# A hybrid decoder layer: the attention pools of the mixer closed early, a pool of its own for the mixed results, and a second mixer that takes two steps at every tenth call

## The chip, the cores and the metric

The kernel runs on one core of one Trainium2 chip. The metric is the device time of one execution in microseconds (us); of several runs the median is given. Engine names: PE is TensorE (matmuls), DVE is VectorE, ACT is ScalarE, POOL is GpSimd, SP is SyncE, which here only issues DMAs.

## The reference

One decoder layer on 1040 tokens (16 meta tokens and 1024 others) of width 1024, all in float32, then a final norm:

```
h = h + 1/2 * SwiGLU(rmsnorm(h))            # FFN 1, hidden width 2816
p = rmsnorm(h) @ w_in                       # q, k, v (512 columns each) and 1024 columns for the convolution
a = diff_attention(q, k, v)                 # 4 heads, two softmax maps each: (p1 - lam * p2) @ v
a = rmsnorm(a, subln_w) * (1 - lambda_init) # per head
c = swish(layernorm(conv31(GLU(u))))        # causal depthwise convolution, 512 channels
h = h + concat([a, c]) @ w_out
h = h + 1/2 * SwiGLU(rmsnorm(h))            # FFN 2
y = rmsnorm(h), without the meta tokens
```

## The kernel before, in words

**Layout.** Activations stand channel by token: 128 partitions of channels, tokens along the free dimension. Tokens are done in two blocks (b = 0: 528 with the meta tokens, b = 1: 512). Every float32 product is made from a high and a low part of both operands (`split`, L128: ACT casts the high part, DVE subtracts it for the low part) as three matmuls: high by high, high by low, low by high. All of them go through `mm` (L57), so they all carry line L58.

**Order.** FFN 1 on block 0, projection of block 0, FFN 1 on block 1 with the mixer of block 0 (attention and convolution) in the background, projection of block 1, FFN 2 on block 0 with the mixer of block 1 in the background, then the output projection of block 1 and FFN 2 on block 1. "In the background" means a generator: `ffn` calls `step()` (L224, L230, L274) between its pieces, and in the two FFNs with a mixer each call takes the generator `bg` one step on (L819, L1017). Two steps are taken ahead (L1015, L1016).

**An FFN.** For each of 22 slices f of the hidden width, `gate_up` (L191) makes 24 matmuls `pg`, calls `step()`, makes 24 matmuls `pu` and calls `step()` again. After each chunk of slices (4, 4, 4, 2, 4, 4 in FFN 2) `down_piece` makes the `dn` matmuls; after each of the four weight tiles of a chunk there is a call of `step()`. One slice of the next chunk is always made ahead of the down pieces. At the start of the last chunk `ahead()` (L253) is called instead; in FFN 2 on block 0 this is `second_out` (L850).

**The mixer (L767).** Its two halves are stepped together. `att` does four heads; each head has four units of 128 queries (`unit`, L417) and each unit has three steps: scores of the first map (`sc`, a PSUM tile of the pool `psS`, which holds one tile); the transposes of the unit before (`tm`, also in `psS`); the product with the values of an earlier pair of units, if there is one, then the scores of the second map and the softmax. When the heads are through and the two pending pieces are done, `sub_ln` (L516) makes the norm of the four heads: squares, four pairs of matmuls `v`, `rstd` (ten small operations), a store of the result row to DRAM (`rscr`, L525), a load that spreads it over all partitions (`ra`, L528), the product (L529) and `store_ac`. `cnv` does the 31 taps of four channel tiles on DVE (L547), then `conv_ln` (L562): sums, two matmuls, `rstd`, and for each tile L585 to L589 and `store_ac`. The taps and the last part of `conv_ln` are given a priority that is lower by 600 instructions (`LATE`); weight loads (`load_w`, L108) are given one that is higher by 500 (`AHEAD`). The framework that builds the program orders the instructions of each engine and each queue by priority and by when it thinks each can start, and an engine then runs its list in that order.

**`store_ac` (L532)** takes one of the eight result tiles (four heads, four convolution tiles), splits it into a high and a low tile (name `a`, 128 x 512, 256 KB each) and stores both to the DRAM scratch `acscr` from POOL (L536). The two tiles come from the tag `rs` of the pool `tmp`, which has two buffers and also serves the temporaries of `rstd`. `ra` comes from the tag `ssum` of the same pool, two buffers.

```
def store_ac(m, i, src):
    hi, lo = [tmp.tile([P, HB], F32R, tag="rs", name="a") for _ in range(2)]
    split(hi, lo, src)
    for j, t in enumerate((hi, lo)):
        store(acscr[m.b, i, :, j], t.bitcast(F32))
```

**`second_out` (L850)** runs what is left of the mixer, closes the mixer's pools, opens others in that memory, and makes the output projection of block 1 in two halves of 256 tokens. Each half needs all eight result tiles: it loads 16 tiles of 256 KB in all from `acscr` (`acl`, and `ext` for four of the second half, L888), the convolution's first, issued by SP as are all weight loads. It then makes, for each half, 8 groups of 24 matmuls `wo` (128 x 256), from eight weight tiles of 512 KB (`wraw<-wo`, then the split `whl`; 2 + 1 and 4 buffers). The first matmuls of each group take the convolution's tiles. The residual comes in one load of 2 MB (`x<-xscr`, L857).

**Pools (L385).** `mid_pools` opens, on the right end of the memory and one above the other, the pools `qk`, `pt`, `v` (all of attention's tiles) and `tmp` (the heads' results and small ones).

Of the kernel before, what the change touches and what calls it, by code (L numbers as in the profile page):

```python
# [9 lines left out]
F32 = mybir.dt.float32  # L10
F32R = mybir.dt.float32r
# [7 lines left out]
P = 128  # L19
# [16 lines left out]
HB = SEQ // 2  # L36
# [3 lines left out]
FB = [[(0, HM // 2), (HM // 2, HM // 2)], [(0, HB)]]  # L40
# [10 lines left out]
def layer(ctx, tc, xb, wgu1, wd1, win, wv, wo, wgu2, wd2, colv, lamv, consts, cossin, out):  # L51
# [5 lines left out]
    def mm(o, lhsT, rhs, start, stop):  # L57
        T.matmul(o, lhsT, rhs, start=start, stop=stop)  # L58

    def pool(stack, name, bufs, side="left"):  # L60
        return stack.enter_context(tc.tile_pool(name=name, bufs=bufs, side=side, reuse_waits="tile"))
# [6 lines left out]
    tmp = pool(ctx, "tmp", 2)  # L68
# [30 lines left out]
    def col(i):  # L99
        return cols[:, i:i + 1]  # L100
# [4 lines left out]
    def psb(name):  # L105
        return psB.tile([P, 512], F32, tag="b", name=name)
# [21 lines left out]
    def split(dst_hi, dst_lo, src):  # L128
        S.copy(dst_hi, src)  # L129
        return V.tensor_tensor(dst_lo, src, dst_hi.bitcast(F32), op=ALU.subtract)  # L130

    def sq_piece(xs, w, ssum, first):
        if first:
            S.activation(ssum[:, :w], xs, AF.Square)
        else:
            sq = tmp.tile([P, 512], F32, tag="sq", name="sq")
            S.activation(sq[:, :w], xs, AF.Square)
            V.tensor_tensor(ssum[:, :w], ssum[:, :w], sq[:, :w], op=ALU.add)
# [7 lines left out]
    def rstd(var, dst, w, scale=1.0, quick=False):  # L146
        def square(o, i):
            if quick:
                V.tensor_tensor(o, i, i, op=ALU.mult)
            else:  # L150
                S.activation(o, i, AF.Square)

        v = tmp.tile([P, 512], F32, tag="rs", name="rv")[:, :w]
        V.tensor_scalar(v, var, scale, EPS, op0=ALU.mult, op1=ALU.add)
        V.tensor_scalar(dst.bitcast(I32), v.bitcast(I32), -0.5, RSQRT_SEED, op0=ALU.mult, op1=ALU.add)
        q = tmp.tile([P, 512], F32, tag="rs", name="rq")[:, :w]
        square(q, dst)
        V.scalar_tensor_tensor(q, q, -RSQRT_K, v, op0=ALU.mult, op1=ALU.mult)
        V.scalar_tensor_tensor(dst, q, RSQRT_K * RSQRT_C, dst, op0=ALU.add, op1=ALU.mult)
        square(q, dst)  # L160
        V.tensor_tensor(v, q, v, op=ALU.mult)
        V.tensor_scalar(q, v, 0.375, -1.25, op0=ALU.mult, op1=ALU.add)
        V.tensor_tensor(q, q, v, op=ALU.mult)
        V.scalar_tensor_tensor(dst, q, 1.875, dst, op0=ALU.add, op1=ALU.mult)

    def norm_r(dst, w, ssum, late=0, extra=None):
        v = psb("v")
        with tc.high_priority(offset=-late):
            mm(v[:, :w], onesD, ssum[:, :w], True, extra is None)
            if extra is not None:  # L170
                mm(v[:, :w], onesD, extra[:, :w], False, True)
        rstd(v[:, :w], dst, w, quick=extra is not None)
# [212 lines left out]
    def mid_pools(stack, b):  # L385
        m = Mid()
        nk = NM + HB * (b + 1)
        m.b, m.nk = b, nk
        m.qk = pool(stack, f"qk{b}", 2, side="right")
        m.pt = pool(stack, f"pt{b}", 2, side="right")  # L390
        m.v = pool(stack, f"v{b}", 2 - b, side="right")
        m.tmp = pool(stack, f"mt{b}", 2, side="right")
        m.vm = m.v.tile([80, P], F32R, tag="vm", name="vm", bufs=1)
        m.pm = [m.tmp.tile([P, 80], F32R, tag=f"pm{i}", name="pm", bufs=1) for i in range(2)]
        for t in m.pm + [m.vm]:
            V.memset(t.bitcast(F32), 0.0)
        load_vm(m, 0)
        m.accs = {}
        m.os = []
        m.pend = []  # L400
        return m

    def load_vm(m, h):
        for part, row in ((0, 0), (0, 32), (1, 64)):
            dma(m.vm[row:row + NM].bitcast(F32), vscr[0:NM, h, part])
# [110 lines left out]
    def sub_ln(m):  # L516
        v = psb("v")
        for h in range(4):
            sq = tmp.tile([P, 512], F32, tag="sq", name="sq")
            S.activation(sq, m.os[h], AF.Square)  # L520
            mm(v[32 * h:32 * h + 32], onesH, sq, True, True)
        rr = tmp.tile([P, 512], F32, tag="ssum", name="rr")
        rstd(v, rr, 512)
        for h in range(4):
            store(rscr[m.b, h:h + 1], rr[32 * h:32 * h + 1])  # L525
        for h in range(4):
            ra = tmp.tile([P, 512], F32, tag="ssum", name="ra")
            dma(ra, rscr[m.b, h].partition_broadcast(P))  # L528
            V.scalar_tensor_tensor(ra, m.os[h], wsub, ra, op0=ALU.mult, op1=ALU.mult)  # L529
            store_ac(m, h, ra)  # L530

    def store_ac(m, i, src):  # L532
        hi, lo = [tmp.tile([P, HB], F32R, tag="rs", name="a") for _ in range(2)]
        split(hi, lo, src)
        for j, t in enumerate((hi, lo)):
            store(acscr[m.b, i, :, j], t.bitcast(F32))  # L536
# [191 lines left out]
    def finish(x, b):  # L728
        todo = []

        def out_piece(c0, w, dd, gained=False):
            for e in (dd, dd + 1):
                y = x[:, e, c0:c0 + w]
                if gained:
                    V.tensor_tensor(y, y, rB[:, c0:c0 + w], op=ALU.mult)
                else:
                    V.scalar_tensor_tensor(y, y, col(C_GF + e), rB[:, c0:c0 + w], op0=ALU.mult, op1=ALU.mult)
            dma(out[dd * P:(dd + 2) * P, b * HB + c0:b * HB + c0 + w].rearrange("(a p) c -> p a c", a=2),
                x[:, dd:dd + 2, c0:c0 + w])

        sums = [None]

        def f(c0, w, d):
            end = b == 1 and c0 + w == HB
            xs = x[:, d, c0:c0 + w]
            if d == 0:
                sums[0] = tmp.tile([P, 512], F32, tag="ssum", name="ssum")
            extra = None
            if end and d == ND - 1:
                extra = tmp.tile([P, 512], F32, tag="sq", name="sq")  # L750
                S.activation(extra[:, :w], xs, AF.Square)
            else:
                sq_piece(xs, w, sums[0], d == 0)
            if todo and d % 2 == 0:
                out_piece(*todo.pop(0))
            if d == ND - 1:
                if end:
                    for e in range(ND):
                        S.activation(x[:, e, c0:c0 + w], x[:, e, c0:c0 + w], AF.Copy, scale=col(C_GF + e))
                norm_r(rB[:, c0:c0 + w], w, sums[0], extra=extra)  # L760
                todo.extend((c0, w, dd, end) for dd in range(0, ND, 2))
                if end or w == HB:
                    for a in todo:
                        out_piece(*a)
        return f

    def mixer(m, zs):  # L767
        def att():
            for h in range(4):
                yield from head(m, h)  # L770
            while m.pend:
                m.pend.pop(0)()
                yield
            sub_ln(m)

        def cnv():
            for c in range(4):
                yield from conv(m, c, zs[c])
            yield from conv_ln(m)
        a, c = att(), cnv()  # L780
        while True:
            done = next(a, STOP) is STOP
            done = (next(c, STOP) is STOP) and done
            if done:
                break
            yield
# [9 lines left out]
    x = ffn1_first()  # L796
# [10 lines left out]
    x = res.pop()  # L807
    enter(xs)
    es_l.close()
    es_m = ExitStack()  # L810
    bg = mixer(mid_pools(es_m, 0), zs)

    def drain():
# [23 lines left out]
    x = res.pop()  # L837
    enter(xs)
    es_l.close()

    es_m = ExitStack()
    bg = mixer(mid_pools(es_m, 1), zs)
    es_l = ExitStack()
    x1 = []
# [169 lines left out]

    next(bg, None)  # L1015
    next(bg, None)  # L1016
    ffn(FB[1], FB[1], wgu2, wd2, x, finish(x, 0), lambda: next(bg, None), third_in, scaled=True, second=True, ahead=second_out)  # L1017
    ffn(FB[1], [(0, QT), (QT, QT)], wgu2, wd2, x1[0], finish(x1[0], 1), nothing, nothing, second=True, pair_of=gate_up_pair)
    es_l.close()

# [73 lines left out]
```

## Time and profile before

| what | us |
|---|---|
| median of 3 runs (1958.42 to 1961.5) | 1961.13 |
| time of the profiled execution | 1960.6 |
| its span | 1958.8 |
| PE busy in it | 1915.6 (98%) |
| DVE busy | 1416.0 (72%) |
| ACT busy | 770.3 (39%) |
| POOL busy | 70.2 (4%) |

The span is the time from the first to the last instruction of the profiled execution; its own time is 1.8 us longer. Busy times are sums over instructions; an engine that is idle is either waiting for another one or has nothing to do. A busy PE may run at a lower clock: the granted clock is given as a share of full speed (2.4 GHz), and its lower level is half of that.

### The profile page before, as it was taken

How to read it: one execution, taken by the hardware profiler on the slowest of the kernel's cores; microseconds unless marked ns; L12 is line 12 of the kernel's file. 1: busy time of each engine (PE TensorE's matmuls, PEld its weight loads, DVE VectorE, ACT ScalarE, POOL GpSimd, SP SyncE). 2: the span in 40 equal slices, each digit the busy share in tenths (PEclk: the TensorE clock that was granted, in tenths of full speed). 3: DMA queues.
4: the chain of work that ended last, by engine and by line, in shares of the span. 5: the costliest groups of instructions: out<-in, count | busy, mean ns of one | idle time of the engine just before them, and what ended most of it. 6: DMA issues, size and time to landing. Idle time of an engine off the chain costs nothing.

```text
span 1958.8 us, 29371 instructions
## 1 busy us (share of the span) xinstructions
PE 1915.6 (98%) x11758; PEld 1705.0 (87%) x11758; DVE 1416.0 (72%) x2220; ACT 770.3 (39%) x1257; POOL 70.2 (4%) x132
## 2 busy tenths in 40 slices
PE   9999999999999999999999999999996999999997
PEld 9999999999988888778878788888785889999997
DVE  8555555677687887766567787888873899777877
ACT  6222222442443343434233454443542445434444
POOL 0000000002200000010002000000011000000000
PEclk9999999999999999999999999999997999999999
DMA  5222232254633432265426632423247534323222
GB/s 172 95 96 87 87 97 87 97 176 154 203 119 100 125 111 89 74 218 177 180 96 179 194 112 87 152 95 100 86 166 269 179 129 152 96 97 101 94 97 66
DMA packets 89001, 249.24 MB, mean 127 GB/s; under 512 B 10928, under 2 KB 26032, under 8 KB 88608
## 3 DMA queue, kind: packets, MB, share of 16 engines
q1 hardware_dynamic: 79888, 217.85, 34.2%
q0 software_dynamic: 8976, 29.52, 4.4%
q8 instruction: 92, 1.51, 0.3%
q14 instruction: 45, 0.37, 0.1%
HBM read 215.72 MB, written 31.61 MB: 126 GB/s over the span
## 4 chain that ended last, share of the span: by engine, by line
PE 88%; DVE 5%; issue 3%; DMA 2%; ACT 1%; POOL 1%; SPq 0%; DVEq 0%; POOLq 0%; ACTq 0%
PE dn L58 22%; PE pg L58 20%; PE pu L58 18%; PE p L976 9%; PE pa L58 5%; PE wo L58 3%; PE pv L58 3%; PE pb L58 2%; PE sc L58 2%; PE o L58 2%; DVE whl L130 1%; DMA acscr<-a 1%; PE tm L477 1%; PE v L58 1%; ACT whl L129 1%
## 5 line engine op out<-in xcount | busy, mean ns | idle before, releaser
L129 ACT CAST whl<-wraw 128x1024 fp32r<-128x1024 f32 (+2 forms) x326 | 334.2, 1026 | 557.8 <-PE dn L58 166.3
L58 PE MATMUL dn<-h,whl 128*128 128x512 f32 (+2 forms) x2736 | 508.9, 345 | 2.4 <-DVE x L242 2.1
L58 PEld LDWEIGHTS dn<-h,whl 128*128 128x128 f32 x2736 | 428.6, 188 | 67.1 <-DVE x L242 2.2
L130 DVE TENSOR_TENSOR whl<-wraw,whl 128x1024 fp32r<-128x1024 f32 (+2 forms) x326 | 388.9, 1193 | 130.7 <-ACT whl L129 128.4
L58 PE MATMUL pg<-xh,whl 128*128 128x264 f32 (+1 forms) x1584 | 410.4, 340 | 3.7 <-ACT xh L143 1.7
L58 PE MATMUL pu<-xh,whl 128*128 128x264 f32 (+1 forms) x1392 | 361.9, 341 | 1.4 <-DVE t L218 1.4
L58 PEld LDWEIGHTS pg<-xh,whl 128*128 128x128 f32 x1584 | 275.1, 189 | 38.3 <-issue 2.6
L58 PEld LDWEIGHTS pu<-xh,whl 128*128 128x128 f32 x1392 | 241.8, 189 | 34.5 <-issue 3.4
L58 PE MATMUL pg<-xl,whl 128*128 128x264 f32 (+1 forms) x792 | 268.0, 340 | 0.7 <-DVE xl L130 0.7
L58 PE MATMUL pu<-xl,whl 128*128 128x264 f32 (+1 forms) x696 | 235.6, 340 | 0.0
L242 DVE SCALAR_TENSOR_TENSOR x<-dn,x 128x512 f32<-128x512 f32 (+2 forms) x248 | 138.8, 569 | 73.3 <-PE dn L58 72.9
L547 DVE SCALAR_TENSOR_TENSOR acc<-z,cols,acc 128x512 f32<-128x512 f32 x240 | 179.2, 747 | 3.4
L58 PEld LDWEIGHTS pg<-xl,whl 128*128 128x128 f32 x792 | 149.1, 189 | 16.6 <-DVE xl L130 1.1
L58 PEld LDWEIGHTS pu<-xl,whl 128*128 128x128 f32 x696 | 130.3, 188 | 15.7 <-issue 1.7
L976 PE MATMUL p<-xh,whl 128*128 128x256 f32 x704 | 128.4, 281 | 0.1
L976 PEld LDWEIGHTS p<-xh,whl 128*128 128x128 f32 x704 | 109.4, 189 | 0.4 <-DVE eg L1006 0.3
L58 PE MATMUL wo<-acl,whl 128*128 128x256 f32 (+1 forms) x480 | 85.5, 339 | 18.5 <-DMA acl<-acscr 18.5
L976 PE MATMUL p<-ext,whl 128*128 128x256 f32 x792 | 98.4, 283 | 2.5 <-ACT whl L129 1.2
L58 PEld LDWEIGHTS wo<-acl,whl 128*128 128x128 f32 x480 | 74.8, 200 | 28.6 <-DMA acl<-acscr 12.6
L976 PEld LDWEIGHTS p<-ext,whl 128*128 128x128 f32 x792 | 95.9, 191 | 4.2 <-ACT whl L129 1.4
L976 PE MATMUL p<-xl,whl 128*128 128x256 f32 x352 | 98.4, 279 | 0.0
L58 PE MATMUL pa<-xh,whl 128*128 128x264 f32 (+2 forms) x384 | 91.1, 322 | 0.0
(196 smaller groups left out, 2188.1 us busy)
## 6 DMA issues: line engine op xcount, KB each, us to landing
wraw<-wgu SPq DMA_DIRECT2D x153, 512.0 KB, 3.3
wraw<-wd SPq DMA_DIRECT2D x72, 512.0 KB, 3.3
wraw<-win SPq DMA_DIRECT2D x32, 512.0 KB, 3.3
wraw<-wo SPq DMA_DIRECT2D x24, 512.0 KB, 3.9
raw<-wgu SPq DMA_DIRECT2D x22, 512.0 KB, 3.3
q<-qscr SPq DMA_DIRECT2D x32, 256.0 KB, 5.9
acscr<-a POOLq DMA_DIRECT2D x32, 256.0 KB, 3.8
wraw<-wd SPq DMA_DIRECT2D x16, 384.0 KB, 3.1
```

Of the source, the lines that this page charges most:

```text
L58: T.matmul(o, lhsT, rhs, start=start, stop=stop)
L129: S.copy(dst_hi, src)
L130: return V.tensor_tensor(dst_lo, src, dst_hi.bitcast(F32), op=ALU.subtract)
L242: last[0] = V.scalar_tensor_tensor(xs, m[:, :w], 0.25, xs, op0=ALU.mult, op1=ALU.add)
L477: T.transpose(tm[:, j], ps_[0][:, o:o + P], ident)
L547: V.scalar_tensor_tensor(a, z[:, j:j + HB], col(wc + j), a, op0=ALU.mult, op1=ALU.add)
L976: T.matmul(o, a, mov[m][b][k], start=first and mat == 0 and k == 0 and i == 0, stop=mat == 1 and k == 3 and i == 2, skip_group_check=True)
```

## The change

The mixer's pools are opened in another order: `tmp` first, then `qk`, `pt` and `v` in a stack of their own. When the last head's pieces are done, that stack is closed and a pool `ao` with eight buffers is opened, before `sub_ln` is called. `sub_ln` takes its four `ra` tiles from it (a tag with four buffers), and `store_ac` its `a` tiles (a tag with eight), for the heads and for the convolution. This holds for the mixers of both blocks. In FFN 2 on block 0 the calls of `step()` take the mixer two steps on at every tenth call; the rest is as it was.

```diff
-        m.qk = pool(stack, f"qk{b}", 2, side="right")
-        m.pt = pool(stack, f"pt{b}", 2, side="right")
-        m.v = pool(stack, f"v{b}", 2 - b, side="right")
+        m.stack, m.es = stack, ExitStack()
         m.tmp = pool(stack, f"mt{b}", 2, side="right")
+        m.qk = pool(m.es, f"qk{b}", 2, side="right")
+        m.pt = pool(m.es, f"pt{b}", 2, side="right")
+        m.v = pool(m.es, f"v{b}", 2 - b, side="right")
+        m.out = None
...
         for h in range(4):
-            ra = tmp.tile([P, 512], F32, tag="ssum", name="ra")
+            ra = m.out.tile([P, 512], F32, tag="ra", name="ra", bufs=4)
...
     def store_ac(m, i, src):
-        hi, lo = [tmp.tile([P, HB], F32R, tag="rs", name="a") for _ in range(2)]
+        hi, lo = [m.out.tile([P, HB], F32R, tag="a", name="a") if m.out else
+                  tmp.tile([P, HB], F32R, tag="rs", name="a") for _ in range(2)]
...
             while m.pend:
                 m.pend.pop(0)()
                 yield
+            m.es.close()
+            m.out = pool(m.stack, f"ao{m.b}", 8, side="right")
             sub_ln(m)
...
-    ffn(FB[1], FB[1], wgu2, wd2, x, finish(x, 0), lambda: next(bg, None), third_in, scaled=True, second=True, ahead=second_out)
+    taken = [0]
+
+    def paced():
+        taken[0] += 1
+        next(bg, None)
+        if taken[0] % 10 == 0:
+            next(bg, None)
+
+    ffn(FB[1], FB[1], wgu2, wd2, x, finish(x, 0), paced, third_in, scaled=True, second=True, ahead=second_out)
```

## Rows read from the trace of the kernel before

**Rows 1.** The profile page: PE's busy tenths in 40 equal slices of the span.

```profile
PE   9999999999999999999999999999996999999997
```

**Rows 2.** PE by stretch: from:to length, busy (instructions), granted clock, DMA share, GB/s.

```profile
1300.00:1447.00 147.00, 147.00 (x699) 1.00 0.30 98
1447.00:1469.40 22.40, 22.38 (x97) 1.00 0.72 241
1469.40:1516.10 46.70, 28.23 (x195) 0.78 0.79 270
1516.10:1574.00 57.90, 56.40 (x339) 1.00 0.50 169
```

**Rows 3.** The matmuls `wo` alone by stretch: PE, PEld, DVE busy, then as above.

```profile
1495.40:1516.10 20.70, 20.70 (x159) 20.48 (x159) 2.93 (x7) 0.89 0.83 275
1516.10:1540.40 24.30, 22.68 (x192) 22.27 (x190) 2.27 (x6) 1.00 0.57 184
```

**Rows 4.** Who waited for whom, 1440 to 1495.4: us in total, times, longest.

```profile
ACT a L129 <- DMA acscr<-a: 19.4, 6, 5.2
...
PE wo L58 <- DMA acl<-acscr: 18.5, 4, 7.1
...
DVE a L130 <- DMA acscr<-a: 13.3, 5, 3.9
```

**Rows 5.** Tiles `a` and `ra`, 1440 to 1500: ns min/median/max, first and last start.

```profile
L529 DVE SCALAR_TENSOR_TENSOR ra<-osb,wsub,ra x4: 744/748/751, 1443.8 to 1459.5; 128x512 f32<-128x512 f32 x4
...
L129 ACT CAST a<-ra x4: 620/621/622, 1444.6 to 1460.3; 128x512 fp32r<-128x512 f32 x4
...
L130 DVE TENSOR_TENSOR a<-acc,a x4: 692/692/693, 1467.3 to 1483.7; 128x512 fp32r<-128x512 f32 x4
...
DMA to landing us min/median/max: 2.3/3.8/6.5
```

**Rows 6.** The chain that ended last, around the last store: start, us, what.

```profile
1484.64 6.54 DMA acscr<-a
1491.23 4.10 DMA acl<-acscr
```

**Rows 7.** Timeline from the last scores to the store of the norm's row.

```profile
1397.66 0.45 PE L58 MATMUL sc<-k,q 128*128 128x512 f32 x1
...
1402.05 0.21 ACT L451 ACTIVATION_READ_ACCUMULATOR p<-sc,nm 128x1 f32 x1
...
1406.77 1.03 PE L477 MATMUL tm<-cst,p 128*128 128x128 f32 x8
...
1415.79 1.05 PE L58 MATMUL v<-sq,onesH 128*32 128x512 f32 x4
...
1437.71 1.94 POOL L525 DMA_DIRECT2D rscr<-rr  x4 [339.16 <-DVE rr L164]
```

**Rows 8.** The chain that ended last: one of the FFN's pieces `pg`.

```profile
1349.87 5.56 PE pg L58 x24
```

**Rows 9.** DVE by stretch: from:to length, busy (instructions), clock, DMA share, GB/s.

```profile
1375.00:1392.00 17.00, 16.62 (x27) 1.00 0.32 114
1392.00:1447.00 55.00, 41.91 (x66) 1.00 0.26 89
1447.00:1469.40 22.40, 13.05 (x18) 1.00 0.72 241
```

**Rows 10.** DMA issues, 1469.4 to 1540: queue, times, KB each, median us to landing.

```profile
acl<-acscr SPq DMA_DIRECT2D x12, 256.0 KB, 4.6
x<-xscr SPq DMA_DIRECT2D x1, 2048.0 KB, 9.7
```

**Rows 11.** The SP queue in order of time: start, us, line, operation.

```profile
1459.58 4.61 SPq L111 DMA_DIRECT2D wraw<-wo  x3
1472.98 0.56 SPq L888 DMA_DIRECT2D acl<-acscr  x1
```

**Rows 12.** Who waited on the SP queue, 1400 to 1545.

```profile
SPq L111 <- DVE whl L130: 57.2, 12, 16.2
```

## The prediction

> **What bounds the kernel now.** I read the page first. PE is busy for 98% of the span, and of the 40 slices one stands out: the 31st, where PE falls to 6 tenths [rows 1]. The table by stretch shows what is to be seen there. Up to 1447 us PE has no gap, and in the last `dn` pieces before the output projection (1447 to 1469.4) none either. Then come 46.7 us that hold 28.2 us of PE work, at a granted clock of 0.78 on the mean, so partly at the lower of its two levels (1.2 GHz, against 2.4), into which it fell while PE stood still; behind it little is left, 1.5 us in 58 [rows 2].
>
> The work in that stretch is the first half of the output projection, 192 matmuls. The second half is the same 192 matmuls at full clock and takes 22.7 us of PE [rows 3]. So the stretch is 46.7 - 22.7 = 24.0 us too long: 18.5 us in which PE is idle, all of it put down to loads of `acl` from the scratch [rows 4], and 28.2 - 22.7 = 5.5 us of slow clock.
>
> Why the loads are late: the chain runs back from them to the last store of an `a` tile, issued at 1484.64 and landed 6.5 us later; the load takes 4.1 us and PE goes on at 1495.4 [rows 6]. The 16 `a` tiles are split from 1444.6 to 1483.7 [rows 5], 39.1 us, of which ACT stood 19.4 us and DVE 13.3 us waiting for stores to land [rows 4]: two buffers serve 16 tiles, so each pair waits for the stores of the pair before (median landing 3.8 us, [rows 5]).
>
> So the price to be won is 24.0 us, and the question is how much later than 1469.4 us the eight result tiles are still ready.
>
> **The paced steps.** From the code: each head is 12 steps, so four heads are 48, the two pending pieces are steps 49 and 50, and `sub_ln` runs in step 51; the convolution's four results leave in steps 51 to 54. With two steps ahead, step 51 falls on call 49 before. Counting the calls (slices 0 to 3 take calls 1 to 8, slice 4 calls 9 and 10, then four for the down pieces, and so on), calls 43 to 46 are the down pieces of the short chunk and call 49 lies between `pg` and `pu` of slice 16. The trace agrees: `v` of `sub_ln` starts at 1415.8 [rows 7], at the end of that `pg`. Afterwards call c has taken 2 + c + c/10 (whole part) steps, so step 51 falls on call 45. Between calls 45 and 49 PE has the last down piece of a chunk of two slices, half of one piece of 5.6 us, and three pieces `pg`, `pu`, `pg` of 5.56 us each [rows 8]: 2.8 + 16.7 = 19.5 us. All that follows from `sub_ln` on is due 19.5 us earlier.
>
> What must keep up is the chain ahead of it: last scores 1397.7, transposes 1406.8, `v` 1415.8, store of the norm's row 1437.7 [rows 7]. That is 40 us, mostly queueing on DVE. Where the steps fall now, during the short down pieces, DVE is busy 16.6 of 17.0 us; then 41.9 of 55 and 13.1 of 22.4 [rows 9]. Up to 1469.4 there are 22.8 us free, and the same work has to fit, only earlier. I take 16 us of the 19.5 as reached, with 19.5 and 8 (half the move lost in DVE's queue) as the ends. The DVE work itself is the same in sum, and so is PE's, so nothing is paid for the move by itself.
>
> **The eight buffers and four `ra`.** Without the waits, the 16 tiles cost ACT 8 x 0.62 = 5.0 us and DVE 8 x 0.69 + 4 x 0.75 (the product with `ra`) = 8.5 us [rows 5]. In a stretch where DVE is 58% busy [rows 9] that is about 8.5 / 0.6 = 14 us. So by the buffers alone the last split would be at 1444.6 + 14 = 1459, landed by 3.8 to 6.5 us later [rows 5], the first load in by another 4.6 [rows 10]: 1467 to 1470, at the very end of the down pieces. By the pace alone the last store lands at 1491.2 - 16 = 1475 [rows 6] and PE goes on at about 1479.5. By both: 1443 for the last split, 1447 to 1450 landed. That is some 20 us of margin.
>
> **What the margin must hold.** The residual (2 MB) and the eight tiles of the first half (8 x 256 KB) are 4.2 MB; at the 241 GB/s seen in the down pieces, or the 275 seen in the busy stretch [rows 3, 9], 15 to 17 us: 1462 to 1467. That just fits. The order of the two may matter. The residual's load takes 9.7 us to land, a tile's load 4.6 [rows 10]; before, it went out behind the first tiles. If it goes out ahead of them, the first `acl` may come up to 9.7 us later: at the latest 1450 + 9.7 + 4.6 = 1464, still before 1469.4; with the lower end of the move (8 us for 16) it would be 1472, and PE would wait some 3 us. No row here shows a tile's load right behind the residual's. The Trainium skill ("DMA: Bandwidth & Descriptors", section "Queues, rings and completion order") says that each DMA engine consumes the descriptors of one queue in ring order, so a tile's load behind the residual on SP would wait for the whole of it; by that rule the late figure of the two holds whenever the residual goes out first, without it the early one, and the sum comes out the same by both.
>
> **The weights of the projection.** Now they are loaded while PE waits; that cover goes. PE uses 8 tiles of 512 KB in 22.7 us; with the 8 tiles of the second half (2.1 MB) and the residual's stores (1 MB) it is 7.3 MB, 322 GB/s, against 275 at which PE did not wait (1495 to 1516, [rows 3]). The second half, with weights alone, ran at 184 GB/s with 1.6 us of gaps [rows 3]. Two or three tiles will be split ahead and as many raw, which is 2 MB less. Bounds: 0 (all hidden, as in the rows) and 7.3 MB / 275 GB/s - 22.7 = 3.9 us. I take 2 us, nearer to the rows in which PE did not wait.
>
> **The doubled steps.** Four calls (10, 20, 30, 40) take two steps; at the fiftieth the mixer is through. Each puts two users of the one-tile pool `psS` one behind the other. From the end of scores to the end of their exponentials, when the tile is free, it took 4.0 us after 1398.1; from scores to the transposes 8.7 us [rows 7]. If other matmuls stand between in PE's list it costs nothing, as now: PE has no gap before 1447 [rows 2], not even where steps fall every 2.8 us. Bounds: 0 and 4 x 8.7 = 34.8 us. I take 1 us in all, since the row nearest to a doubled step is the stretch with a step every 2.8 us, and it has no gap.
>
> **Edits at nothing.** Closing the attention pools and opening `ao` on their place: an `a` tile waits for the readers of keys, queries and probabilities, which are all behind the last head's result, and `sub_ln` needs that result anyway. The tiles opened later on `ao`'s place (`ext`, some `acl`) wait for the last stores, which these loads wait for already. Four `ra` loads on SP instead of two and two: they wait for the row's store in one place, ahead of weight loads that have to wait for PE there as it is (SP waited 57.2 us in sum for the split of weights, [rows 12]). Block 0: its results are wanted one whole projection later; PE does not wait for them, so nothing.
>
> **Sum.** 24.0 - 2 - 1 = 21.0 us. The profiled execution took 1960.6 us (span 1958.8 and 1.8 around it): 1939.6. The median of the runs is 0.5 above it: 1940.
>
> **Rivals.**
> A, the forecast: the stall goes and little comes back. All of it: 1936.6 + 0.5 = 1937; with the 1.5 us behind it 1935.5; with the upper bound of the weights (3.9) and one doubled step at 4.0 us, 1945. Its own range 1935 to 1945. Chance 0.67.
>
> B, the SP queue keeps the loads back. SP takes its list in order, and loads of `wo` weights wait for free buffers: it stood at `wraw<-wo` until 1464 and issued the first `acl` at 1472.98 [rows 11], the longest such wait being 16.2 us [rows 12]. If the `acl` loads are still listed behind these, the stores' earlier end helps only in part: first tile in at 1473 + 4.6 = 1477.6, 8.2 us of idle PE and about 5 of slow clock and late weights: 13 of 24 us stay, so 1950. For it: the waits are long. Against it: at 1472.98 the load itself was still waiting for stores. Chance 0.16.
>
> C, the results come no earlier. The last part of the convolution has a priority lower by 600, so its tiles could stay where they are, at 1467 to 1484 [rows 5]: 1958 to 1962. Against it: what they waited for was the buffers [rows 4]. Chance 0.09.
>
> D, slower: the doubled steps stop PE. Place: the four calls; price: 8.7 us each if nothing stands between, 34.8 in all, so 1940 - 1 + 34.8 = 1974. It decides from (21 + 1 + 4) / 4 = 6.5 us per doubled step on; at 4.0 us each it would be 1955. A sentence apart: the Trainium skill ("PSUM — Partial Sum Buffer") says that matmuls start and complete in program order, so one that waits for `psS` holds back all behind it; by that alone D's price would be paid in full wherever the list has nothing between. That the list mixes in other matmuls is what speaks against it. Chance 0.08.
>
> **How the numbers follow.** A measurement of this kernel can tell a change of 0.2%, 4 us, from none: below 1957 is faster, above 1965 slower. A and B are faster, 0.83; C is no change, 0.09; D slower, 0.08. The range takes A and B's middle: 1935 to 1952.
>
> **What would show it.** Right: PE's 31st slice at 9, no wait of PE for `acl` above 3 us, no wait of ACT or DVE for stores of `a` above some 5 us in sum, the last store of `a` before 1455, clock 1.0 throughout. B: SP's first `acl` load after 1465 while the last store landed long before. C: the last store after 1475. D: gaps of PE ahead of `sc` or `tm` between 1100 and 1370, where there were none. I would be wrong in the sum if PE waits for the weights of the projection by more than 4 us.

## The result, and the profile after

The changed kernel takes 1939.17 us (median of 4 runs, 1936.23 to 1940.39) against 1961.32 of the kernel before (4 runs): a ratio of 0.9885, 95% interval 0.9865 to 0.9904. The forecast was 1940, in a range of 1935 to 1952, and faster. The profiled execution is the fastest of the four, 1936.23 us, with a span of 1934.5 us, 24.3 less than before.

The page's slices first (PE's busy tenths and the granted clock), where before the 31st slice stood at 6 [rows 1]:

```profile
PE   9999999999999999999999999999999999999997
PEclk9999999999999999999999999999999999999999
```

The stretches of PE in the changed kernel (from:to, length, busy, clock, DMA share, GB/s):

```profile
1060.00:1375.00 315.00, 312.50 (x1608) 1.00 0.40 127
1375.00:1447.00 72.00, 72.00 (x325) 1.00 0.47 157
1447.00:1469.40 22.40, 22.40 (x100) 1.00 0.94 330
1469.40:1516.10 46.70, 45.64 (x387) 1.00 0.69 231
```

The 46.7 us that held 28.2 us of PE work at a clock of 0.78 [rows 2] now hold 45.6 at full clock, both halves of the output projection; the missing 1.1 us is a wait of PE for DVE behind them, ahead of the next `pg`. The traffic has moved ahead: the `dn` pieces run at 330 GB/s and a DMA share of 0.94, against 241 and 0.72.

The results leave earlier. The tile `a` in the changed kernel (ns min/median/max, first and last start; the line numbers have shifted by a few), to be held against [rows 5]:

```profile
L539 POOL DMA_DIRECT2D acscr<-a x16: 539/540/581, 1431.0 to 1445.4; - x16
L129 ACT CAST a<-ra x4: 621/623/625, 1430.1 to 1435.5; 128x512 fp32r<-128x512 f32 x4
...
L130 DVE TENSOR_TENSOR a<-acc,a x4: 682/683/693, 1440.1 to 1444.2; 128x512 fp32r<-128x512 f32 x4
...
DMA to landing us min/median/max: 2.3/4.6/13.6
```

The first of the 16 splits starts at 1430.1 and the last at 1444.2, 14.1 us later instead of 39.1, and the last store goes out at 1445.4 instead of 1484.6 [rows 6]. One number is worse: a store took up to 13.6 us to land. The timeline of the changed kernel (start, length, engine, what) shows the steps of [rows 7], and why:

```profile
1382.10 0.45 PE L58 MATMUL sc<-k,q 128*128 128x512 f32 x1
...
1402.75 1.05 PE L58 MATMUL v<-sq,onesH 128*32 128x512 f32 x4
...
1423.47 1.95 POOL L527 DMA_DIRECT2D rscr<-rr  x4 [324.16 <-DVE rr L164]
...
1444.88 0.33 SPq L862 DMA_DIRECT2D x<-xscr  x1
1446.61 2.97 SPq L111 DMA_DIRECT2D wraw<-wo  x2
1449.68 10.61 SPq L893 DMA_DIRECT2D acl<-acscr  x5
...
1468.93 6.24 PE L58 MATMUL wo<-acl,whl 128*128 128x256 f32 x52
```

The last scores are 15.6 us earlier, `v` of `sub_ln` 13.0, the store of the norm's row 14.2. The residual's 2 MB now go out at 1444.88, with the last stores and ahead of all tiles. PE goes from `dn` to `wo` with no wait that the trace records.

### The profile page after: what moved, and what is told of

It is laid out like the page before. It is cut to its first block, busy times and chain, and to the rows that moved or that the text cites. A ratio compares the mean times of both kernels' runs of the same rounds, so it can differ in the third digit from the quotient of the medians.

```text
span 1934.5 us, 29349 instructions
## 1 busy us (share of the span) xinstructions
PE 1910.6 (99%) x11758; PEld 1700.5 (88%) x11758; DVE 1415.1 (73%) x2220; ACT 769.5 (40%) x1257; POOL 70.2 (4%) x132
## 4 chain that ended last, share of the span: by engine, by line
PE 89%; DVE 5%; DMA 3%; issue 1%; ACT 1%; POOL 0%; SPq 0%; DVEq 0%; ACTq 0%; POOLq 0%
PE dn L58 23%; PE pg L58 21%; PE pu L58 18%; PE p L981 9%; PE pa L58 5%; PE pv L58 3%; PE pb L58 2%; PE wo L58 2%; PE sc L58 2%; PE o L58 2%; DMA wraw<-wo 1%; DVE whl L130 1%; PE tm L479 1%; PE v L58 1%; ACT whl L129 1%
## 5 line engine op out<-in xcount | busy, mean ns | idle before, releaser
L129 ACT CAST h<-t 128x512 fp32r<-128x512 f32 (+1 forms) x110 | 58.5, 534 | 57.4 <-DVE t L228 54.1
L228 DVE TENSOR_TENSOR t<-pu,t 128x264 f32<-128x264 f32 (+1 forms) x87 | 48.8, 562 | 44.2 <-PE pu L58 42.1
```

The lines of the kernel that those rows point to most:

```text
L228: V.tensor_tensor(tw, pu, tw, op=ALU.mult)
```

## The experiments

The experiments were run in three groups, each beside its own runs of the kernel before: e1 to e4 (before at 1961.70 us), c1, e5, e7 and e8 (1961.71), and c2, e6, e9 and e10 (1960.72). c1 and c2 are the changed kernel run again. A ratio is taken to these, with its 95% interval in brackets.

### Which part earns what: the buffers alone, the pace alone

e1_buffers_only is the changed kernel without the doubled step:

```diff
-        if taken[0] % 10 == 0:
-            next(bg, None)
```

> The changed pools without the doubled steps. Theory (each part does about half, and the stall needs both): results come 16 to 19 us later than in the changed kernel, the last split near 1460 us, the last store landed near 1465. SP's list here has the residual's load and the first two acl loads ahead of the last weight tiles of the down pieces, so PE would wait in or right behind the dn pieces, 8 to 14 us with slow clock: 1946 to 1953. Rival 1 (the buffers alone carry the gain): 1937 to 1941, no PE wait over 3 us from 1440 to 1520. Rival 2 (the pace alone carries it): 1957 to 1962, PE still waiting 15 us or more for acl.

e2_pace_only is the kernel before with `paced` in place of the one step per call:

```diff
-... lambda: next(bg, None), third_in, ...
+... paced, third_in, ...
```

> The doubled steps with the pools of before. Theory: everything from the norm of the heads on is 14 to 19 us earlier, but the 16 tiles still take about 39 us through two buffers: last store landed near 1472 to 1477, PE goes on near 1480, waits 8 to 12 us for acl, clock below 1.0 for a few us: 1946 to 1953. Rival 1 (buffers alone carry the gain): 1957 to 1962. Rival 2 (pace alone carries it): 1937 to 1941.

Measured: e1 1946.71 us, ratio 0.9923 [0.9909, 0.9936]; e2 1947.55, ratio 0.9924 [0.9911, 0.9938]. PE's wait for the loads (us in total, times, longest) in e1, then in e2:

```profile
PE wo L58 <- DMA acl<-acscr: 4.4, 1, 4.4
```

```profile
PE wo L58 <- DMA acl<-acscr: 10.3, 2, 8.9
```

The stretches of PE in e1, then in e2:

```profile
1469.40:1485.00 15.60, 11.22 (x72) 0.89 0.93 332
```

```profile
1469.40:1485.00 15.60, 5.34 (x36) 0.80 0.93 333
1485.00:1516.10 31.10, 31.10 (x249) 0.94 0.79 257
```

Each part alone wins 15.0 and 14.2 us, both together 21.6 to 23.6 (c1, c2 and the first runs of the changed kernel): each moves the results by enough to win more than half of the 24 us, and once the results are in before the `dn` pieces end, having them earlier is worth nothing, so the two do not add up. Neither rival holds. Of e1's expectation the time came true, but not the way to it: SP sent the weights of the down pieces out first, PE waited 4.4 us at the first `wo`, and with the slow clock behind it the stretch from the first `dn` to the last `wo` piece took 72.2 us, 6.2 more than in the changed kernel, not 8 to 14. Another 2.0 us went to a wait of PE for DVE behind the projection. e2's last store was issued at 1469.9 and landed at 1476.8, inside the expected 1472 to 1477; the load behind it took 6.5 us, and PE went on at 1483.4, later than the expected 1480.

### Whether the pace alone can do it

e9_fifth_only is e2 with `taken[0] % 5` in place of `% 10`.

> The pools of before with two steps at every fifth call, so the norm falls on call 41 instead of 45. With every tenth call and two buffers the last store was issued at 1469.9 and PE waited 10.3 us. Theory (only the time at which the results are stored counts, however it is won): some 10 us earlier again, last store near 1460, PE waits 0 to 3 us for acl, 1936 to 1941, without any new pool. Rival (two buffers keep the stall): PE waits 6 us or more, 1944 or above.

Measured: 1937.84 us, ratio 0.9886 [0.9871, 0.9902], the time of the changed kernel, with the pools of before. Tile `a`, and PE in the stretch that had held the stall:

```profile
L536 POOL DMA_DIRECT2D acscr<-a x16: 539/539/581, 1414.9 to 1452.9; - x16
```

```profile
1469.40:1516.10 46.70, 46.70 (x393) 1.00 0.69 229
```

Two buffers still need 38 us for 16 tiles, but from 1414.9 on. The last store is issued at 1452.9, 17.0 us earlier than in e2, where 10 were expected, and PE waits for no load of `acl`. What counts here is when the last tile is stored, however that is won; the new pools are not needed for this gain.

### What a doubled step costs

e3_every_fifth is the changed kernel with `% 5` in place of `% 10`.

> The changed kernel with two steps at every fifth call: eight doubled steps ahead of the norm instead of four, which then falls on call 41. Theory (a doubled step costs PE nothing, other matmuls stand between): within 2 us of the changed kernel, 1937 to 1941, no new PE gap between 1100 and 1375. Rival (each doubled step stops PE for 4.0 us, the time from scores to a free tile): 16 us more than the changed kernel, 1953 to 1957, with gaps ahead of sc or tm.

Measured: 1937.18 us, ratio 0.9873 [0.9860, 0.9887]. PE by stretch in it:

```profile
1060.00:1375.00 315.00, 312.50 (x1611) 1.00 0.40 127
```

The same 312.50 us of PE work as in the changed kernel with half as many doubled steps, and 311.65 in the kernel before with none. PE waited for `sc` once in that stretch, 0.2 us. A doubled step costs PE nothing that shows here.

### What the residual's place on SP does

e4_residual_last issues the residual's load behind the eight tiles of the first half:

```diff
-        dma(t, xscr[1])
...
-                    dma(a.bitcast(F32), acscr[1, i, :, :, c])
+                    got = dma(a.bitcast(F32), acscr[1, i, :, :, c])
                     srcs.append(a)
+                if q == 0:
+                    with tc.issue_after(got.ins):
+                        dma(t, xscr[1])
```

> The changed kernel, with the 2 MB load of the residual issued on SP behind the eight tiles of the first half instead of ahead of them. In the changed kernel the first acl loads took up to 10.8 us to land, the last stores of a up to 13.6. Theory (they queue behind the residual's data): the first acl loads land in 4 to 6 us and the last stores in under 8; PE did not wait for them, so the time stays, 1937 to 1941. Rival (the engines are simply full, whatever the order): the first acl loads still take 9 us or more.

Measured: 1937.27 us, ratio 0.9874 [0.9861, 0.9888]. The stores of tile `a` in the changed kernel took up to 13.6 us to land, as shown above; in e4 (us min/median/max):

```profile
DMA to landing us min/median/max: 2.3/4.0/6.3
```

The loads of `acl`, in the changed kernel and then in e4:

```profile
DMA to landing us min/median/max: 3.5/6.5/10.8
```

```profile
DMA to landing us min/median/max: 4.8/5.5/6.6
```

The order decides: with the residual behind, the slowest store lands in 6.3 us instead of 13.6 and the slowest tile in 6.6 instead of 10.8. PE had not waited for them, so the time stays.

e8_buffers_residual_last is e4 without the doubled steps.

> The changed pools, no doubled steps, and the residual's 2 MB load behind the eight tiles of the first half. With the buffers alone and the residual ahead, the last split was at 1461.6 us, the first acl was issued at 1464.5 and PE waited 4.4 us for one, on till 1476. Theory (what the pace buys is the time that the tiles lose behind the residual): first tiles in some 5 us after their issue, PE waits 0 to 2 us for acl, 1938 to 1942, within 3 us of the changed kernel. Rival (the results are simply too late without the pace): PE waits 4 us or more, 1944 to 1948.

Measured: 1949.12 us, ratio 0.9938 [0.9924, 0.9951]. The theory falls. The rival holds in the wait, 4.3 us of PE for `acl`; the time is 1.1 us above its range. The chain that ended last in e8:

```profile
1464.77 5.96 DMA acscr<-a
...
1472.65 6.17 DMA acl<-acscr
...
1478.86 12.36 PE wo L58 x81
```

PE is through with `dn` at about 1473.8. Even with nothing large ahead of it, a tile stored at 1464.8 has landed at 1470.7 and is loaded again at 1478.8. Without the pace the results are too late by 4 to 5 us in either order of the loads. The order is not without effect: e8 takes 76.1 us from the first `dn` to the last `wo` piece, 3.9 more than e1, with a second wait of 2.0 us in the second half of the projection.

### How many buffers, and which

e7_four_a has four `a` buffers instead of eight; e6_ra_from_tmp takes `ra` from the two old buffers:

```diff
-            m.out = pool(m.stack, f"ao{m.b}", 8, side="right")
+            m.out = pool(m.stack, f"ao{m.b}", 4, side="right")
```

```diff
-            ra = m.out.tile([P, 512], F32, tag="ra", name="ra", bufs=4)
+            ra = tmp.tile([P, 512], F32, tag="ssum", name="ra")
```

> The changed kernel with four buffers for the a tiles instead of eight. Theory (a tile's turn costs its split and a landing of about 4 us, so four buffers give 16 tiles in about 20 us where two took 38 and eight 14): last store issued about 1450, 5 to 6 us later than with eight; the loads then land close to the end of the dn pieces: 0 to 3 us of waits, 1937 to 1942. Rival (fewer than eight puts the stall back): PE waits 5 us or more for acl, 1944 or above.

> The changed kernel with the ra tiles in the two buffers of before; only the a tiles have the new pool. Theory (the waits were those of the a tiles): within 2 us of the changed kernel, last store at most 5 us later. Rival (ra counts as much): last store 10 us later or more, PE waits for acl.

c1_changed_again and c2_changed_third are the changed kernel, run beside them.

> The changed kernel itself, to stand beside the next three on the same chip: 1936 to 1941.

> The changed kernel itself once more, to stand beside the next three on the same chip: 1936 to 1941.

Measured: e7 1940.17 us (0.9892 [0.9879, 0.9906]) beside c1 1938.09 (0.9881 [0.9868, 0.9895]); e6 1941.03 (0.9904 [0.9888, 0.9920]) beside c2 1939.10 (0.9893 [0.9877, 0.9910]). PE waits for `acl` in neither. The stores of e6, then of c2:

```profile
L539 POOL DMA_DIRECT2D acscr<-a x16: 539/539/578, 1434.8 to 1452.7; - x16
```

```profile
L539 POOL DMA_DIRECT2D acscr<-a x16: 539/539/578, 1435.3 to 1448.7; - x16
```

The last store is 4.0 us later with `ra` in two buffers. In e7 it goes out at 1454.8, 7.0 us later than in c1, where 5 to 6 were expected. Both differ from the changed kernel by some 2 us in the median, with intervals that overlap. In the stage itself the profiles show no such cost: from the first `dn` to the last `wo` piece e7 takes 66.0 us, as the changed kernel does, and e6 66.4. Behind it PE waits for DVE, 3.0 us in e7 and 1.6 in e6, against 1.1 in the changed kernel's first profile and nothing in c1 and c2. Whether fewer buffers cause that stays open. The large step is from e2, with two buffers of each (1947.55 us), to four of `a`.

e5_fifth_residual_last joins e3 and e4.

> Two steps at every fifth call and the residual last, both on top of the changed kernel. Theory (PE no longer waits here, so more margin buys nothing): within 2 us of the changed kernel. Rival (some loss is left in this stage that margin removes): 2 to 4 us less than the changed kernel.

Measured: 1938.19 us, 0.9881 [0.9867, 0.9894], the same as c1. More margin in this stage buys nothing. All profiles say the same: where the last store was issued by 1454.8 (the changed kernel, e3 to e7, e9, e10), PE waited for no `acl`; at 1463.2 (e1) and 1464.8 (e8) it waited 4.4 and 4.3 us, at 1469.9 (e2) 10.3 and at 1484.6 (before) 18.5.

### A wait that the new order brings, and a version that beats both

One stretch of PE far ahead of the change's stage got longer: from a long down piece of FFN 1 on block 0 (322 us in the kernel before) to the first `dn` piece of FFN 1 on block 1 (582 us) it takes 259.9 us in the three kernels with the old pools (before, e2, e9), and 262.4 to 266.7 in all ten executions with the new pools. In each of these ten PE waits for `q` of block 0 near 535 us, 2.4 to 3.8 us in nine, and in the changed kernel's first profile 0.3, with 1.6 more soon after, for which the profile shows no releaser; in the other three it doesn't. e10_block1_only keeps block 0's pools as before:

```diff
+        if b == 1:
+            m.tmp = pool(stack, f"mt{b}", 2, side="right")
+        on = m.es if b == 1 else stack
+        m.qk = pool(on, f"qk{b}", 2, side="right")
...
+        if b == 0:
+            m.tmp = pool(stack, f"mt{b}", 2, side="right")
...
+            ra = m.out.tile([P, 512], F32, tag="ra", name="ra", bufs=4) if m.out else tmp.tile([P, 512], F32, tag="ssum", name="ra")
...
+            if m.b == 1:
+                m.es.close()
+                m.out = pool(m.stack, f"ao{m.b}", 8, side="right")
```

> The changed kernel, but the mixer of block 0 keeps its pools as before (order, buffers); only block 1 has the new ones. In the kernels with the new order the first q and k of block 0 are loaded at 530 us instead of 486, because their place in memory is free later, and PE waits 1.6 to 3.7 us for q ahead of the first scores; before, and with the pace only, it does not. Theory (the new order costs block 0 this wait): no PE wait for q between 500 and 560, first loads of q near 486, time 2 to 3 us less than the changed kernel, 1934 to 1937. Rival (the wait is hidden elsewhere later): same time as the changed kernel.

Measured: 1932.10 us (4 runs, 1931.82 to 1932.75), ratio 0.9858 [0.9843, 0.9873], beside 1939.10 of the changed kernel (1937.98 to 1940.33). It beats both. In c2, the waits on the SP queue (us in total, times, longest):

```profile
SPq L412 <- DMA vscr<-ve: 6.8, 1, 6.8
```

and the SP queue's timeline in c2 (start, length):

```profile
530.40 0.33 SPq L412 DMA_DIRECT2D k<-kscr  x1
530.83 0.62 SPq L415 DMA_DIRECT2D q<-qscr  x1
```

and in e10, where there is no such wait:

```profile
471.47 0.86 SPq L416 DMA_DIRECT2D k<-kscr  x2
...
484.93 3.01 SPq L419 DMA_DIRECT2D q<-qscr  x4
```

PE's timeline in c2 (in brackets the idle time ahead and what ended it):

```profile
321.29 17.71 PE L58 MATMUL dn<-h,whl 128*128 128x264 f32 x144
...
539.30 0.49 PE L58 MATMUL sc<-k,q 128*128 128x144 f32 x1 [3.03 <-DMA q<-qscr]
...
587.43 5.71 PE L58 MATMUL dn<-h,whl 128*128 128x512 f32 x24
...
1450.65 22.36 PE L58 MATMUL dn<-h,whl 128*128 128x512 f32 x96
...
1516.69 1.56 PE L58 MATMUL wo<-acl,whl 128*128 128x256 f32 x12
```

and in e10:

```profile
321.00 17.71 PE L58 MATMUL dn<-h,whl 128*128 128x264 f32 x144
...
580.91 5.71 PE L58 MATMUL dn<-h,whl 128*128 128x512 f32 x24
...
1445.41 22.37 PE L58 MATMUL dn<-h,whl 128*128 128x512 f32 x96
...
1511.45 1.56 PE L58 MATMUL wo<-acl,whl 128*128 128x256 f32 x12
```

The stretch of the wait and the 5 us right behind it in c2, and then the stretch in e10 (from:to, length, PE busy, clock, DMA share, GB/s):

```profile
520.00:545.00 25.00, 21.97 (x85) 0.88 0.74 212
540.00:545.00 5.00, 5.00 (x13) 0.50 0.99 194
```

```profile
520.00:545.00 25.00, 25.00 (x115) 1.00 0.58 191
```

In c2 the load of `k` goes out 59 us later than in e10, and `q` behind it. 6.8 us of that it waits for the stores of the projection's `ve` tiles; the rest is its later place in SP's list. From the code: `k` takes nothing from `vscr`, so the wait is for a place in memory; with `tmp` opened first, `qk` of block 0 lies on another place, where `ve` tiles had been. PE waits 3.0 us, and behind that the granted clock is at its lower level (0.50 from 540 to 545 us).

The stretch from 321 us to the first `dn` piece of block 1 takes 587.43 - 321.29 = 266.1 us in c2 and 580.91 - 321.00 = 259.9 in e10: the wait costs 6.2 us, twice its idle time, since the clock of 0.88 over 25 us takes some 3 more. By 1447 us the lead is 5.2 us; 0.3 of it e10 had at 321, and 1.3 were given back on the way. Between 582 and 1447 us all ten executions with the new pools were a little quicker (862.4 to 863.6 us) than before, e2 and e9 (865.0 to 866.3); e10 lies between them with 864.5. Two waits of PE make most of that, for `q` of block 1 near 1114 and ahead of a `dn` piece for DVE: 2.0 us together in the kernel before, 2.5 in e2, 2.6 in e9, 1.6 in e10 and at most 0.2 in the ten. Why the ten are without them stays open. So e9, with no wait in block 0, is no faster than the changed kernel. From the first `dn` to the last `wo` piece c2 and e10 both take 66.0 us. The remaining 2 us of e10's gain arise behind the output projection (the spans are 1937.4 and 1930.2). Some 1.8 of them are clock: from 1580 to 1600 us it is granted at 0.91 in c2 and at 1.00 in e10. It is at 1.00 there in e4 and e6 too, which have the new pools in block 0, so nothing ties this part to e10's edit. The profiles show 5.2 us as e10's own; the medians differ by 7.0. The expectation had the place and the cause, but put the gain at 2 to 3 us, for the idle time alone.

## Why the prediction was right, and where it was not

**The size of the stall: right.** From the first `dn` piece to the last `wo` piece it took 1537.30 - 1447.01 = 90.3 us before, and 66.0 in all three profiles of the changed kernel: 24.3 us, against 24.0 worked out from the stretch.

**The move by the pace: right, a little less than taken.** 16 us were taken for all that follows from `sub_ln` on, with 8 and 19.5 as the ends; `v` moved by 13.0, the norm's row by 14.2, the first split by 14.5. That nothing is paid for the doubled steps on PE holds by e3; the 1 us set aside was not needed.

**The 16 tiles in 14 us: right**, 14.8 measured from the first split's start to the last one's end. The forecasts for one part alone had the splits and stores right and the landings too short. By the buffers alone the last split was forecast at 1459 and measured to end at 1462.3 in e1, where the whole timeline stood 2.8 us later (first `dn` at 1449.8); but the first tile was forecast in by 1467 to 1470, and e1's, issued at 1464.5 behind the residual, landed 11.9 us later, at 1476.4. By the pace alone the last store was forecast landed at 1475 and landed at 1476.8 in e2; the load behind it took 6.5 us, where 4 to 5 were counted, and PE went on at 1483.4, not at 1479.5.

**The margin: too large.** "Some 20 us" rested on stores that land in 3.8 to 6.5 us. The residual went out with the last stores and ahead of all tiles, stores took up to 13.6 us and tiles up to 10.8. The last store landed at 1459.0, 10 us ahead of `wo`; the first tile was in at 1460.4, between the two figures (1454.6 and 1464), and the last of the first half's eight at 1468.7, where 1462 to 1467 had been worked out. PE did not wait, but much less was left than forecast. The Trainium skill ("DMA: Bandwidth & Descriptors", "Queues, rings and completion order") has each DMA engine take one queue's descriptors in ring order. The trace agrees for the tiles, which share SP's queue with the residual: it landed at 1456.4, the two tiles issued ahead of its landing at 1460.4 and 1461.2, and in e4, where the first eight tiles went out ahead of it, they took 5.3 to 6.1 us. The stores are on another queue and were slowed as well, which that rule does not cover.

**The weights: taken at 2 us, measured at none.** From the first `dn` to the last `wo` piece PE never waits in the changed kernel's three profiles. The 7.3 MB that made 322 GB/s held 2 MB that the prediction itself expected to be fetched earlier; without them it is 5.3 MB in 22.7 us, 233 GB/s, below the 275 at which PE had not waited. The `dn` stretch took up 330 GB/s, and from 1485 to 1516 us the changed kernel moved 184 GB/s.

**Block 0 at nothing: wrong.** The prediction named its results, which nobody waits for, and not its first loads: the new order of the pools moved `qk` onto a place that is free later. That cost 2.5 us in the changed kernel's first profile and 6.2 to 6.4 in c1 and c2, of which some 2 came back before the `dn` pieces. So the path in the stage was right, but that the sum met the median within 1 us is partly luck: the 3 us set aside for weights and doubled steps, which were not needed, covered most of what block 0 cost.

**The rivals.** B (the SP queue holds the loads back) did not come about: `acl` went out at 1449.7, not after 1465. C and D are excluded by the times of the stores and by e3. One reading under them was wrong: "PE has no gap before 1447" was taken from a row that starts at 1300. Between 1060 and 1375 the kernel before has 3.3 us of gaps, one of them 1.2 us ahead of `sc` at 1114, so a gap there would have been no sign of D by itself.

## What to carry to other kernels

A chain of store, landing and load again ends on a deadline: count back from the first consumer to the time by which the last tile must be stored, and make the chain end by then. Here an earlier start alone was enough (e9) and eight buffers alone were not (e1); more than the deadline asks bought nothing (e5). When pools are put in another order, look at every tile whose place moves, in every block that uses them: the first load onto a place waits for the last user of what lay there, as `k` in c2 did for the stores of `ve`. And do not price a short wait of PE by its idle time alone: in c2 3.0 us of it cost 6.2. Read the granted clock behind it.

## What the runs showed of the hardware that was not expected

A 2 MB load on SP's queue slowed 256 KB stores that POOL had issued: at most 13.6 us to land with it among them, 6.3 with it behind (the changed kernel and e4). Other profiles agree: the slowest store took 12.3 to 13.1 us in c1, c2, e1, e6 and e10, where the residual went out among the last stores, and 6.2 to 7.0 in e5 and e8, where it went out behind the tiles. After PE's waits of 2.4 to 3.8 us for `q` near 535 us the granted clock stood at 0.86 to 0.95 in the mean of the 25 us around them, in all nine executions; in the one where PE stood still for 0.3 and then, 7 us later, for 1.6 us it stayed at 1.00. Among the three profiles of the changed kernel this alone makes 3.7 to 3.9 us in the stretch from 321 us to the first `dn` piece of block 1. Whether it also makes the 4 us by which the other executions of this program differ, of which no trace is kept, is not shown.
